# Table stores issued by ScalarE, the output tile of a table block as a step of its own, and the split of y one scan step later

## The chip, the cores and the metric

The kernel runs on one core of one Trainium2 chip. The metric is the device time of one execution in microseconds (us). A core has five engines that each run their own instructions in order: TensorE (PE in the profile; PEld is its weight load), VectorE (DVE), ScalarE (ACT), GpSimd (POOL) and SyncE (SP). They meet through semaphores. Transfers are issued by SP, ScalarE or GpSimd and run on DMA engines that the whole core shares.

## The reference

A decoder trunk of two layers on x of 256 positions by 2048 features in float32. Each layer ends in `layer_norm(alpha * x + mixer(x))`.

```
def ssd_moba_mixer(x, w_in, conv_w, conv_b, dt_bias, a_log, d_skip, norm_g, w_out):   # layer 0
    z, xbc, dt, q, k, v, gate = jnp.split(x @ w_in, SPLITS0, axis=-1)
    ...                                   # conv, chunked state-space scan, RMSNorm -> y_a
    y_b = moba_attention(q, k, v).reshape(bsz, s, ATT_WIDTH) * jax.nn.silu(gate)
    return jnp.concatenate([y_a, y_b], axis=-1) @ w_out

def s5_ssm(u, lam_re, lam_im, log_dt, b_re, b_im, c_re, c_im, d_skip):
    lam = lax.complex(lam_re, lam_im); dt = jnp.exp(log_dt)[:, None]
    lam_bar = jnp.exp(lam * dt)
    b_bar = ((lam_bar - 1.0) / lam)[..., None] * lax.complex(b_re, b_im)
    c_mat = lax.complex(c_re, c_im)
    def step(h, u_blk):                   # 128 groups of 16 channels, 64 complex states each
        bu = jnp.einsum('gnm,blgm->blgn', b_bar, u_blk)
        bu = bu.at[:, 0].add(lam_bar * h)
        _, hs = lax.associative_scan(_linear_recurrence, (lam_bar, bu), axis=1)
        return hs[:, -1], jnp.einsum('gmn,blgn->blgm', c_mat, hs).real
    ...
    return y + d_skip * u

def s5_mixer(x, w_in, ..., w_glu, w_out):                                              # layer 1
    u, gate = jnp.split(x @ w_in, 2, axis=-1)
    y = jax.nn.gelu(s5_ssm(u, ...))
    ga, gb = jnp.split(y @ w_glu, 2, axis=-1)
    return ((ga * jax.nn.sigmoid(gb)) * jax.nn.silu(gate)) @ w_out
```

## The kernel before

**Products.** The time goes into five large products (`wi0`, `wo0`, `wi1`, `wglu`, `wo1`). [...] Weights come in units of 128 partitions by 1024 float32 (512 KB). SP loads a unit into `raw` (L222), ScalarE makes the upper part `wh` (L225) and VectorE the remainder `wl` (L227). There are four buffers of each, and `split_to` prepares units up to three ahead of the one that TensorE works on. The matmuls of the products stand at L271 (one unit is 12 of them, 512 columns each) and L288 (24 of them, 256 columns each). The large tiles that hold split activations have the one-letter names A, B, C, D, F.

**Side work.** All else is cut into small jobs. `pump`, called after each unit, takes some of them. Jobs in the queue `jobs` are spread over the product at hand; jobs in the queue `back` are spread evenly over the units up to a unit number, `goal`. So a job more in `back` changes beside which unit the later ones are issued. The order on each engine is then settled by a scheduler that simulates the kernel's times; an engine executes its own list strictly in that order.

**Scan tables, made during layer 0.** Layer 1 needs tables for its scan that depend on parameters alone. They are built in 16 blocks, b = 0 to 15, as jobs in `back`, in `block_jobs(b)`, and go to DRAM, into `wb[b]`:

- `bars` loads the parameters (L650) and makes `bb`.
- `efs` makes `et` (L676 to L679, VectorE) and, in the same job, the second half of the output tile `ob` (L684 to L686, VectorE). `ob` has two buffers, so the tile of block b can be written only after the store of block b−2 has landed.
- `pes` transposes `et` on TensorE (L694, with 16 small matmuls at L698), copies the result into the first half of `ob` on ScalarE (L699), makes `kt` on VectorE (L704, L705) and stores `ob` (L706, 512 KB), issued by GpSimd.
- `mts`, for odd b, makes `om` from `kt` on TensorE (L713), VectorE (L715) and ScalarE (L717) and stores its two halves (L719, 128 KB each), issued by GpSimd.

GpSimd also computes a table of phasors for each block (L627 to L640), a chain of small products (L630, L635, L637, L638) that ends with a store of its own (L640). The blocks run beside the attention and the output product of layer 0. At the end of layer 0 comes a LayerNorm whose four column quarters are normalized (L1010, L1013), transposed on TensorE (L358) and split on ScalarE (L1023) and VectorE (L1027), while the first product of layer 1 has begun.

**The scan in layer 1.** A list of steps, `at(t, f)`, is spread over the units of the first product of layer 1. For block b it loads the tables (L1111, step 2b−2), encodes on TensorE (L1128, step 2b), rotates on VectorE (up to L1146), scans there (L1153, L1155, L1156), decodes on TensorE (L1169, L1173, step 2b+3), applies GELU on ScalarE (L1179) and stores to `yd` (L1184, L1185). u goes through DRAM: `u_store` (L1083, L1084) writes a quarter of it and `u_load` (L1094, L1095) reads it back in another layout as `um`. y comes back the same way: when the four blocks of a quarter are done, `y_load` (L1198) reads it into a tile and `y_split` divides it into upper part (L1206, ScalarE, into A) and remainder (L1207, VectorE, into B). The tile of `y_load` and that of `u_store` are one buffer (tag `ut`).

Of the kernel before, what the change touches and what calls it, by code (L numbers as in the profile page):

```python
# [9 lines left out]
F32 = mybir.dt.float32  # L10
# [6 lines left out]
P = 128  # L17
# [142 lines left out]
def trunk(tc, io, out):  # L160
    nc = tc.nc
# [3 lines left out]
    def nm(s):  # L165
        count[0] += 1
        return f"{s}_{count[0]}"

    with ExitStack() as top:
# [10 lines left out]
        def C(name):  # L180
            lo, hi = CONST[name]
            return ct[:, lo:hi]

        def PR(name):
            lo, hi = PARAM[name]
            return pt[:, lo:hi]
# [3 lines left out]
        def aux():  # L190
            return auxp.tile([P, 512], F32, tag="aux", name=nm("aux"))

        def big(tag, shape, dt=F32):
            return slot.tile(shape, dt, tag=tag, name=nm(tag))
# [176 lines left out]
        wb = [dram.tile([P, 1792], F32, name=f"wb{b}") for b in range(16)]  # L371
# [9 lines left out]
        with ExitStack() as l0:  # L381
            wk = l0.enter_context(tc.tile_pool(name="wk", bufs=1))
            pp = l0.enter_context(tc.tile_pool(name="pp", bufs=1))
# [260 lines left out]
            def block_jobs(b):  # L644
                h = {}
                gs = slice(8 * b, 8 * b + 8)

                def bars():
                    bc = h["bc"] = pp.tile([P, 4, 8, 16], F32, tag="bc", name=nm("bc"))
                    nc.sync.dma_start(bc.rearrange("p a g m -> p (a g m)"), io["s5bc"][b].rearrange("p a g m -> p (a g m)"))  # L650
                    bb = h["bb"] = pp.tile([P, 3, 8, 16], F32, tag="bb", name=nm("bb"))
                    tm = pp.tile([P, 512], F32, tag="tm", name=nm("tm"))
                    tv = tm.rearrange("p (a g m) -> p a g m", a=4, g=8)
                    wr = wri[:, 0, gs].unsqueeze(2).to_broadcast([P, 8, 16])
                    wi = wri[:, 1, gs].unsqueeze(2).to_broadcast([P, 8, 16])
                    V.tensor_tensor(bb[:, 0], bc[:, 0], wr, op=OP.mult)
                    V.tensor_tensor(tv[:, 0], bc[:, 1], wi, op=OP.mult)
                    V.scalar_tensor_tensor(bb[:, 1], bc[:, 1], sgn, wr, op0=OP.mult, op1=OP.mult)
                    V.scalar_tensor_tensor(tv[:, 1], bc[:, 0], sgn, wi, op0=OP.mult, op1=OP.mult)
                    V.tensor_tensor(bb[:, 0], bb[:, 0], tv[:, 0], op=OP.add)  # L660
                    V.tensor_tensor(bb[:, 1], bb[:, 1], tv[:, 1], op=OP.subtract)
                    V.tensor_scalar(bb[:, 2], bc[:, 2], nsg, None, op0=OP.mult)

                def lk(i, k):
                    return lam[:, i, gs, k - 1].unsqueeze(2).to_broadcast([P, 8, 16])

                def fk(i):
                    return lap[:, i, 4 * b : 4 * b + 4, :].unsqueeze(2).to_broadcast([P, 4, 16, 4])

                def efs():  # L670
                    bc, bb = h["bc"], h["bb"]
                    et = h["et"] = pp.tile([P, 8, 16, 4], F32, tag="et", name=nm("et"))
                    tm = pp.tile([P, 8, 16, 4], F32, tag="tm", name=nm("tm"))
                    ob = h["ob"] = pp.tile([P, 1024], F32, tag="ob", bufs=2, name=nm("ob"))
                    for s in range(3):
                        V.tensor_tensor(et[:, :, :, s], bb[:, 0], lk(0, 3 - s), op=OP.mult)  # L676
                        V.tensor_tensor(tm[:, :, :, s], bb[:, 1], lk(1, 3 - s), op=OP.mult)
                    V.tensor_tensor(et[:, :, :, 0:3], et[:, :, :, 0:3], tm[:, :, :, 0:3], op=OP.add)
                    V.tensor_copy(et[:, :, :, 3], bb[:, 0])  # L679
                    cp = [bc[:, 3, 4 * i : 4 * i + 4, :].unsqueeze(3).to_broadcast([P, 4, 16, 4]) for i in range(2)]  # L680
                    for r in range(2):
                        fv = ob[:, 512 + 256 * r : 768 + 256 * r].rearrange("p (g m t) -> p g m t", g=4, m=16)
                        tm = pp.tile([P, 4, 16, 4], F32, tag="tm", name=nm("tm"))
                        V.tensor_tensor(fv, cp[0], fk(r), op=OP.mult)  # L684
                        V.tensor_tensor(tm, cp[1], fk(1 - r), op=OP.mult)
                        V.tensor_tensor(fv, fv, tm, op=OP.add if r else OP.subtract)  # L686

                def pes():
                    et, ob, bb = h["et"], h["ob"], h["bb"]
                    ev = et.rearrange("p (a i) m s -> p a (i m s)", i=2)  # L690
                    cv = bb[:, 2].rearrange("p (a i) m -> p a i m", i=2)
                    pe, pk = aux(), aux()
                    for a in range(4):
                        T.transpose(pe[:, a * P : a * P + P], ev[:, a, :], ident)  # L694
                    for a in range(4):
                        for i in range(2):
                            at = 64 * (i ^ (a % 2))
                            T.matmul(pk[at : at + 64, a * 16 : a * 16 + 16], ev[:, a, 64 * i : 64 * i + 64], cv[:, a, i, :], start=True, stop=True)  # L698
                    A.activation(ob[:, 0:512], pe, AF.Copy)  # L699
                    if b % 2 == 0:  # L700
                        ktp[0] = pp.tile([P, 8, 16], F32, tag="kt", name=nm("kt"))
                    kt = ktp[0][:, 4 * (b % 2) : 4 * (b % 2) + 4, :]
                    dc = PR("s5d")[:, 4 * b : 4 * b + 4].unsqueeze(2).to_broadcast([P, 4, 16])
                    V.tensor_tensor(kt, C("kmask").unsqueeze(1).to_broadcast([P, 4, 16]), dc, op=OP.mult)  # L704
                    V.tensor_tensor(kt, pk[:, 0:64].rearrange("p (a m) -> p a m", m=16), kt, op=OP.add)  # L705
                    nc.gpsimd.dma_start(wb[b][:, 0:1024], ob)  # L706

                def mts():
                    kf = ktp[0].rearrange("p a m -> p (a m)")
                    pm = aux()  # L710
                    om = pp.tile([P, 512], F32, tag="om", name=nm("om"))
                    for j in range(3):
                        T.matmul(pm[:, j * 128 : j * 128 + 128], C("shift")[:, j * P : j * P + P], kf, start=True, stop=True)  # L713
                    mv = om.rearrange("p (k t) -> p t k", t=4)
                    V.tensor_copy(mv[:, 3, :], kf)  # L715
                    for j in range(3):
                        A.activation(mv[:, 2 - j, :], pm[:, j * 128 : j * 128 + 128], AF.Copy)  # L717
                    for i in range(2):
                        nc.gpsimd.dma_start(wb[b - 1 + i][:, 1024:1280], om[:, 256 * i : 256 * i + 256])  # L719

                return [bars, efs, pes, mts] if b % 2 else [bars, efs, pes]

            jobs.extend([trig_job, table_job])
            xs = big("C", [P, 2, D])
# [344 lines left out]
        with ExitStack() as l1:  # L1069
# [18 lines left out]
            def u_load(hh):  # L1088
                j, h = hh // 2, hh % 2
                u = um[hh] = w1("um", [P, 12, 64], 3)  # L1090
                for i in range(2):
                    src = ud[j][16 * h + 8 * i : 16 * h + 8 * i + 8].rearrange("q a c -> a q c")
                    at = 64 * (1 - i)
                    nc.gpsimd.dma_start(u[64 * i : 64 * i + 64, 0:8, :], src)  # L1094
                    nc.gpsimd.dma_start(u[at : at + 64, 8:12, :], src[:, 1::2, :])  # L1095
# [3 lines left out]
            def at(t, f):  # L1099
                steps.setdefault(t, []).append(f)  # L1100
# [99 lines left out]
            def y_split(j):  # L1200
                if j == 0:
                    y5["h"] = big("A", [P, KT, S], F32R)
                    y5["l"] = big("B", [P, KT, S], F32R)
                yt = y5[j]
                fs = slice(4 * j, 4 * j + 4)
                A.activation(y5["h"][:, fs, :], yt, AF.Copy)  # L1206
                V.tensor_tensor(y5["l"][:, fs, :], yt, y5["h"][:, fs, :].bitcast(F32), op=OP.subtract)  # L1207

            for b in range(16):
                ssm(b)  # L1210
                if b % 2 == 0:
                    at(2 * b - 2, lambda b=b: u_load(b // 2))
                if b % 4 == 3:
                    at(2 * b + 6, lambda b=b: y_load(b // 4))
                    at(2 * b + 8, lambda b=b: y_split(b // 4))
            sg1 = wk.tile([P, 2, D], F32, tag="sg1", bufs=1, name="sg1")
            for j in range(8):
                ps = product("w" if j < 4 else "x", x1hl) if j else first1
# [105 lines left out]
```

## Time and profile before

| | |
|---|---|
| median of 3 runs | 1374.88 us |
| lowest and highest run | 1372.33 and 1376.38 us |
| profiled execution, its own time | 1374.04 us |
| its span | 1372.3 us |
| TensorE busy | 1351.2 us (98%) |
| VectorE busy | 980.6 us (71%) |
| ScalarE busy | 673.5 us (49%) |
| GpSimd busy | 372.2 us (27%) |
| issued by SP (q1) | 239.33 MB |
| issued by GpSimd (q0) | 40.90 MB |
| issued by ScalarE (q10) | 1.18 MB |

How to read the rows that follow. A row of the timeline is: start in us, duration in us, engine, line of the kernel, instruction, output<-inputs, sizes, how many times, and in brackets how long the engine had been idle and what released it. Matmuls are pipelined, so their durations overlap and one reads the distance from start to start. A row of the waits is: engine, output and line, what it waited for, then us in total, times, and the longest. A row of the windows is: the stretch in us, its length, then busy time and number of instructions of PE, PEld, DVE, ACT and POOL, then TensorE's granted clock (1.00 is full speed), the DMA engines' busy share and GB/s. A row of the chain that ended last is: start, duration, and what the chain went through there. In a group of one line's instructions, three durations are minimum, median and maximum in ns. A row of the DMA issues ends with the size and the median time from issue to landing in us.

### The profile page before, as it was taken

The page shows a single profiled execution, that of the slowest core. Times are in us where ns is not written, and L with a number is a line of the kernel's source. Part 1 is how long each engine was busy: PE and PEld are TensorE (multiplying, and loading weights), DVE is VectorE, ACT ScalarE, POOL GpSimd, SP SyncE. Part 2 cuts the span into 40 slices and gives each one's busy share as a digit, 9 for nine tenths or more (in the row PEclk, how much of TensorE's full clock was granted, in tenths as well). Part 3 has the DMA queues.
Part 4 walks back from the last instruction along what each step waited for, and adds up shares of the span by engine and source line. Part 5 has one row for each costly group of instructions (what it writes and reads, how often), then busy time and mean ns, then how long its engine had stood idle before and what let it go on. Part 6 is the DMA issues. An engine that isn't in the chain of part 4 may idle for free.

```text
span 1372.3 us, 25096 instructions
## 1 busy us (share of the span) xinstructions
PE 1351.2 (98%) x9918; PEld 1216.1 (89%) x9918; DVE 980.6 (71%) x1559; ACT 673.5 (49%) x869; POOL 372.2 (27%) x681
## 2 busy tenths in 40 slices
PE   9999999999999999999999899999999999999996
PEld 9999999998998998998988788899877788888885
DVE  5788746787688789779877766748878856555665
ACT  5565557754544544544554344344345545444441
POOL 0140000122016637737888200013333200000001
PEclk9999999999999999999999999999999999999998
DMA  8556655445546756755866678498889766666772
GB/s 304 179 156 197 182 169 155 160 146 171 174 150 209 240 175 214 234 182 190 278 193 194 221 226 305 143 304 264 278 225 303 219 207 186 197 184 187 256 216 77
DMA packets 79206, 283.02 MB, mean 206 GB/s; under 512 B 9840, under 2 KB 10480, under 8 KB 78576
## 3 DMA queue, kind: packets, MB, share of 16 engines
q1 hardware_dynamic: 68112, 239.33, 56.1%
q0 software_dynamic: 10400, 40.90, 8.8%
q8 instruction: 78, 1.28, 0.4%
q10 hardware_dynamic: 576, 1.18, 0.2%
q14 instruction: 40, 0.33, 0.1%
HBM read 260.41 MB, written 20.97 MB: 205 GB/s over the span
## 4 chain that ended last, share of the span: by engine, by line
PE 85%; POOL 7%; DVE 3%; DMA 2%; issue 2%; ACT 0%; POOLq 0%
PE main L288 42%; PE main L271 35%; POOL c L635 3%; POOL c L637 1%; POOL c L638 1%; DMA wb<-c 1%; PE aux L358 1%; DVE wl L227 1%; PE aux L791 1%; PE enc L1128 1%; PE dec L1173 1%; PE aux L367 1%; DMA ut<-yd 1%; PE aux L761 0%; PE aux L698 0%
## 5 line engine op out<-in xcount | busy, mean ns | idle before, releaser
L227 DVE TENSOR_TENSOR wl<-raw,wh 128x1024 fp32r<-128x1024 f32 x431 | 537.3, 1248 | 334.7 <-ACT wh L225 328.7
L225 ACT ACTIVATE wh<-raw 128x1024 fp32r<-128x1024 f32 x431 | 455.8, 1059 | 581.0 <-PE main L271 270.7
L288 PE MATMUL main<-A,wh 128*128 128x256 f32 x1408 | 402.5, 286 | 0.0
L288 PE MATMUL main<-A,wl 128*128 128x256 f32 x1408 | 400.1, 284 | 0.0
L288 PE MATMUL main<-B,wh 128*128 128x256 f32 x1408 | 399.8, 284 | 0.0
L288 PEld LDWEIGHTS main<-A,wh 128*128 128x128 f32 x1408 | 270.5, 192 | 0.6 <-issue 0.2
L288 PEld LDWEIGHTS main<-B,wh 128*128 128x128 f32 x1408 | 270.5, 192 | 0.4
L288 PEld LDWEIGHTS main<-A,wl 128*128 128x128 f32 x1408 | 270.5, 192 | 0.3 <-issue 0.2
L271 PE MATMUL main<-wh,A 128*128 128x512 f32 x512 | 201.5, 394 | 0.0
L271 PE MATMUL main<-wh,B 128*128 128x512 f32 x512 | 201.1, 393 | 0.0
L271 PE MATMUL main<-wl,A 128*128 128x512 f32 x512 | 200.9, 392 | 0.0
L271 PE MATMUL main<-wh,C 128*128 128x512 f32 x384 | 152.4, 398 | 0.0
L271 PE MATMUL main<-wh,F 128*128 128x512 f32 x384 | 150.5, 392 | 0.0
L271 PE MATMUL main<-wl,C 128*128 128x512 f32 x384 | 150.3, 391 | 0.0
L271 PEld LDWEIGHTS main<-wh,B 128*128 128x128 f32 x512 | 96.7, 189 | 20.2
L271 PEld LDWEIGHTS main<-wl,A 128*128 128x128 f32 x512 | 96.8, 189 | 20.0 <-issue 0.2
L271 PEld LDWEIGHTS main<-wh,A 128*128 128x128 f32 x512 | 96.7, 189 | 19.9 <-issue 0.2
L635 POOL TENSOR_TENSOR c<-c 128x8 f32<-128x8 f32 (+2 forms) x192 | 99.3, 535 | 19.2 <-DMA wb<-c 11.8
L271 PEld LDWEIGHTS main<-wh,C 128*128 128x128 f32 x384 | 72.5, 189 | 15.7
L271 PEld LDWEIGHTS main<-wh,F 128*128 128x128 f32 x384 | 72.4, 188 | 15.3
L271 PEld LDWEIGHTS main<-wl,C 128*128 128x128 f32 x384 | 72.5, 189 | 14.5
L801 POOL TENSOR_TENSOR ssq<-ssq,c 128x256 f32<-128x256 f32 x16 | 17.6, 1100 | 210.2 <-ACT c L799 209.6
(281 smaller groups left out, 1690.0 us busy)
## 6 DMA issues: line engine op xcount, KB each, us to landing
raw<-in_wi SPq DMA_DIRECT2D x271, 512.0 KB, 4.1
raw<-in_wo SPq DMA_DIRECT2D x96, 512.0 KB, 4.3
raw<-in_wglu SPq DMA_DIRECT2D x64, 512.0 KB, 3.7
wt<-wb POOLq DMA_DIRECT2D x16, 896.0 KB, 8.1
wb<-ob POOLq DMA_DIRECT2D x16, 512.0 KB, 6.0
bc<-in_s5bc SPq DMA_DIRECT2D x16, 256.0 KB, 4.2
wb<-c POOLq DMA_DIRECT2D x16, 256.0 KB, 3.6
wb<-om POOLq DMA_DIRECT2D x16, 128.0 KB, 3.4
```

The source lines that it names most:

```text
L225: high = A.activation(wh, raw, AF.Copy)
L227: splits[n] = (high, V.tensor_tensor(wl, raw, wh.bitcast(F32), op=OP.subtract))
L271: T.matmul(ps[o], l[:, k, sl], r[:, j, :], start=start and i == 0, stop=stop and i == 2)
L288: T.matmul(pv[o // 2][:, o % 2, :], l[:, j, sl], r[:, k, :], start=first and i == 0 and o % 2 == 0, stop=end and i == 2 and o % 2 == 1, sk ...
L358: end = T.transpose(dst[:, i * P : i * P + P], s, ident)
L367: T.matmul(px[:64, 0:64], idle, idle, start=i == 0, stop=i == n - 1)
L635: G.tensor_tensor(p[:, :, :, 0:m], cs[:, :, :, 1 : m + 1], cs[:, i, :, n : n + 1].unsqueeze(1).to_broadcast([P, 2, 4, m]), op=OP.mult)
L637: G.tensor_tensor(cs[:, 0, :, n + 1 : n + 1 + m], p0[:, 0, :, 0:m], p1[:, 1, :, 0:m], op=OP.subtract)
L638: G.tensor_tensor(cs[:, 1, :, n + 1 : n + 1 + m], p0[:, 1, :, 0:m], p1[:, 0, :, 0:m], op=OP.add)
L791: T.matmul(yo, xs[:, 0, xc], df[:, i, 0:256], start=True, stop=False)
L801: G.tensor_tensor(ssq, ssq, jk[:, f, :], op=OP.add)
L1128: T.matmul(px[64 * at : 64 * at + 64, i, r * 128 + q * 64 : r * 128 + q * 64 + 64], wt[64 * i : 64 * i + 64, a * P + 64 * r : a * P + 64 * ...
```

## The change

Three edits. The stores of `ob` (L706) and `om` (L719) are issued by ScalarE instead of GpSimd; the phasors' store L640 stays on GpSimd. The part of `efs` that makes the second half of `ob` becomes a job of its own, `fcs`, between `efs` and `pes`, so that the tile is taken there; 16 more jobs stand in `back` with that, 97 instead of 81, up to the same unit. `y_split` moves from step 2b+8 to 2b+9 of the scan's list. No arithmetic changes. The diff:

```diff
@@ efs, in block_jobs
                     tm = pp.tile([P, 8, 16, 4], F32, tag="tm", name=nm("tm"))
-                    ob = h["ob"] = pp.tile([P, 1024], F32, tag="ob", bufs=2, name=nm("ob"))
                     for s in range(3):
                         V.tensor_tensor(et[:, :, :, s], bb[:, 0], lk(0, 3 - s), op=OP.mult)
                         V.tensor_tensor(tm[:, :, :, s], bb[:, 1], lk(1, 3 - s), op=OP.mult)
                     V.tensor_tensor(et[:, :, :, 0:3], et[:, :, :, 0:3], tm[:, :, :, 0:3], op=OP.add)
                     V.tensor_copy(et[:, :, :, 3], bb[:, 0])
+
+                def fcs():
+                    bc = h["bc"]
+                    ob = h["ob"] = pp.tile([P, 1024], F32, tag="ob", bufs=2, name=nm("ob"))
                     cp = [bc[:, 3, 4 * i : 4 * i + 4, :].unsqueeze(3).to_broadcast([P, 4, 16, 4]) for i in range(2)]
                     for r in range(2):
                         fv = ob[:, 512 + 256 * r : 768 + 256 * r].rearrange("p (g m t) -> p g m t", g=4, m=16)
@@ pes
-                    nc.gpsimd.dma_start(wb[b][:, 0:1024], ob)
+                    nc.scalar.dma_start(wb[b][:, 0:1024], ob)
@@ mts
                     for i in range(2):
-                        nc.gpsimd.dma_start(wb[b - 1 + i][:, 1024:1280], om[:, 256 * i : 256 * i + 256])
-
-                return [bars, efs, pes, mts] if b % 2 else [bars, efs, pes]
+                        nc.scalar.dma_start(wb[b - 1 + i][:, 1024:1280], om[:, 256 * i : 256 * i + 256])
+
+                return [bars, efs, fcs, pes, mts] if b % 2 else [bars, efs, fcs, pes]
@@ layer 1
                 if b % 4 == 3:
                     at(2 * b + 6, lambda b=b: y_load(b // 4))
-                    at(2 * b + 8, lambda b=b: y_split(b // 4))
+                    at(2 * b + 9, lambda b=b: y_split(b // 4))
```

Lines of the kernel before are given throughout the prediction; from `fcs` on those of the changed kernel are three higher.

## The prediction

> **What bounds the kernel now.** I read the page's busy shares first, then the waits, then a table of windows, and last the timeline around each wait of TensorE (PE).
>
> ```profile
> span 1372.3 us, 25096 instructions
> PE 1351.2 (98%) x9918; PEld 1216.1 (89%) x9918; DVE 980.6 (71%) x1559; ACT 673.5 (49%) x869; POOL 372.2 (27%) x681
> ACT wh L225 <- PE main L271: 270.7, 167, 6.8
> PE dec L1173 <- DVE gt L1155: 2.9, 1, 2.9
> 750.00:775.00 25.00, 20.87 (x97) 16.80 (x96) 13.65 (x24) 7.78 (x10) 12.63 (x33) 0.86 0.74 253
> 1000.00:1025.00 25.00, 22.08 (x231) 16.81 (x231) 21.95 (x32) 12.66 (x15) 7.77 (x15) 0.93 0.77 236
> ```
>
> PE is busy for 98% of the span. ScalarE (ACT), which makes the upper half `wh` of every weight unit, mostly waits for PE to hand a buffer back (270.7 us in 167 waits), so time is gained only where PE stops or runs slowly. In the middle of the kernel there are two such places, one in each of the two windows shown: PE is busy 20.87 and 22.08 us of 25, and its mean granted clock (the column behind POOL) is 0.86 and 0.93. The change touches what stands behind both.
>
> **Part 1: the stores and the split of `efs`.** The first place, in the timeline, with two rows of the chain of waits at the end:
>
> ```profile
> 737.99 0.39 PE L271 MATMUL main<-wh,C 128*128 128x512 f32 x1
> 738.86 0.60 ACT L699 ACTIVATE ob<-aux 128x512 f32<-128x512 f32 x1 [1.64 <-PE aux L694]
> 739.33 0.50 PE L271 MATMUL main<-wl,C 128*128 128x512 f32 x1
> 739.99 0.42 DVE L686 TENSOR_TENSOR ob<-ob,tm 128x256 f32<-128x256 f32 x1
> 750.66 0.55 POOL L706 DMA_DIRECT2D wb<-ob  x1
> 754.65 0.39 PE L271 MATMUL main<-wh,B 128*128 128x512 f32 x1
> 756.72 1.58 DVE L684 TENSOR_TENSOR ob<-bc,lap 128x256 f32<-128x256 f32 x2 [5.11 <-DMA wb<-ob]
> 758.23 0.80 DVE L678 TENSOR_TENSOR et<-et,tm 128x384 f32<-128x384 f32 x1
> 759.17 1.05 PE L694 MATMUL aux<-consts,et 128*128 128x128 f32 x4 [4.13 <-DVE et L678]
> 761.13 0.80 PE L271 MATMUL main<-wh,A 128*128 128x512 f32 x1
> 766.25 0.40 PE L271 MATMUL main<-wh,A 128*128 128x512 f32 x1
> 750.66 6.04 DMA wb<-ob
> 818.36 49.92 PE main L271 x220
> ```
>
> The `ob` of one block is complete at 739.99+0.42 = 740.41, but GpSimd (POOL), which works through its phasor products in order, issues the store at 750.66: 10.25 us of queue, then 6.04 us of transfer. VectorE (DVE) stands at the next write into that buffer (L684) for 5.11 us, and the planner has put L684 ahead of L678, the sum that completes `et`. So L678 is late, PE's transposes L694 wait 4.13 us, and afterwards PE runs at about half clock.
>
> Price: from the last product matmul before the table group to the first after it takes 761.13−754.65 = 6.48 us; the same group without a wait takes 739.33−737.99 = 1.34; so 5.14 us. Then 12 product matmuls take 766.25−761.13 = 5.12 us; at the 49.92/220 = 0.227 us of the long run they take 2.72; so 2.40. Together **7.54 us**.
>
> After: ScalarE issues the store when its own L699 (738.86+0.60) and VectorE's L686 are done, at about 740.4. Even with the 6.04 us of before it lands at 746.5. VectorE comes to L684 at 756.72−5.11 = 751.6: 5 us of slack, so the wait goes. The split cures it a second way, since the new step starts after `et` is complete and a late buffer no longer delays L678. Next late in that group would be L678 itself, done 0.8 us after the end of L677, before PE gets there. I take all 7.54.
>
> **Part 2: `y_split` one step later.** The second place, again with one row of the chain at the end:
>
> ```profile
> 990.65 0.39 PE L271 MATMUL main<-wh,F 128*128 128x512 f32 x1
> 991.07 1.06 ACT L225 ACTIVATE wh<-raw 128x1024 fp32r<-128x1024 f32 x1 [1.66 <-PE main L271]
> 991.36 0.75 POOL L1198 DMA_DIRECT2D ut<-yd  x1 [5.81 <-DMA ud<-ut]
> 991.82 0.50 PE L271 MATMUL main<-wh,C 128*128 128x512 f32 x1
> 998.89 1.06 ACT L1206 ACTIVATE A<-ut 128x1024 fp32r<-128x1024 f32 x1 [6.76 <-DMA ut<-yd]
> 1000.74 0.39 PE L271 MATMUL main<-wh,F 128*128 128x512 f32 x1
> 1005.50 0.79 PE L271 MATMUL main<-wh,C 128*128 128x512 f32 x1
> 1008.54 0.39 PE L271 MATMUL main<-wl,C 128*128 128x512 f32 x1
> 991.36 7.50 DMA ut<-yd
> ```
>
> The load of the first quarter of y is issued at 991.36 and lands at 998.86. ScalarE has stood at its split L1206 for 6.76 us by then, with the weight splits L225 queued behind it; VectorE's half L1207 and the scan's L1155 come later still, and PE's L1173 waits 2.92 us. Price: 1005.50−1000.74 = 4.76 against 991.82−990.65 = 1.17 for the like group, so 3.59; then 7 matmuls in 1008.54−1005.50 = 3.04 against 7×0.227 = 1.59, so 1.45. Together **5.04 us**.
>
> After: in the changed order two more weight splits stand ahead of L1206 on ScalarE. They come at PE's pace of 12×0.227 = 2.72 us, at 993.8 and 996.5, so ScalarE reaches L1206 at about 997.6 and waits 1.3 us instead of 6.76. What is queued behind is the next `wh`; the buffers ahead hold 3×2.72 us of PE's work, less 1.06 for `wh` and 1.22 for `wl`, so 5.9 us of cover. L1155 stands ahead of L1207 on VectorE now. The wait of PE goes; I take all 5.04.
>
> **Part 3: what is new.**
>
> ```profile
> L1299 ACTq DMA_DIRECT2D out_x<-D x4: 338/338/377, 1355.4 to 1368.3; - x4
> DMA to landing us min/median/max: 3.7/6.0/7.8
> POOL wb L706 <- DVE kt L705: 53.7, 3, 24.3
> 873.52 0.44 PE L358 MATMUL aux<-consts,D 128*128 128x128 f32 x2 [1.27 <-DVE D L1013]
> 875.00:879.00 4.00, 4.00 (x23) 4.00 (x22) 3.54 (x6) 0.36 (x1) 0.00 (x0) 0.57 0.00 0
> 882.44 1.04 PE L358 MATMUL aux<-consts,D 128*128 128x128 f32 x8
> 883.80 1.22 DVE L227 TENSOR_TENSOR wl<-raw,wh 128x1024 fp32r<-128x1024 f32 x1
> 884.93 0.68 DVE L1027 TENSOR_TENSOR F<-aux,C 128x512 fp32r<-128x512 f32 x1
> 979.94 0.96 PE main L288 x8
> 912.14 0.72 POOL L1094 DMA_DIRECT2D um<-ud  x1 [4.98 <-DMA ud<-ut]
> 920.50 0.32 PE L1128 MATMUL enc<-um,wt 64*64 64x64 f32 x2
> um<-ud POOLq DMA_DIRECT2D x16, 128.0 KB, 6.2
> ```
>
> *Issue on ScalarE.* 16 table stores and 16 small ones at 0.34 us each (first row, ScalarE's own issue) are 10.8 us on an engine at 49%; the 1.66 us of idle before a weight split takes one. Path cost 0. Without that cover it would be 10.8. GpSimd loses the same 32 issues, which are on no path; only its wait for kt (third row, 53.7 us) goes with them.
>
> *Wait on ScalarE.* The store waits for VectorE's L686 (about 1 us in the rows of Part 1) and has L225 queued behind it; cover 5.9 us; cost 0. The trace has no large store on ScalarE's queue: 3.7 to 7.8 us to landing (second row, the table stores on GpSimd's) are the nearest bounds, and with any of them the buffer is free in time.
>
> *Layer 0's LayerNorm tail.* The 16 additional steps shift the planner's order at 882 us: all 8 transposes L358 come after 48 product matmuls, and the product then needs the fourth L1027, which stands on VectorE behind the `wl` of a unit whose `wh` waits for the last of these matmuls. That chain is 1.06 (`wh`) + 1.22 + 0.68 = 3.0 us against 1.04 of transposes and two matmuls at 0.96/8 = 0.12 (the row at 979.94, of the chain) of cover: a wait of about 1.7 us that is not there now, less some 0.3 from transposes that move behind matmuls: +1.4. A wait of 1.27 us at 873.52 was followed by a clock of 0.57 over 4 us, a loss of 4×0.43 = 1.7. Loss of clock 0 to 1.7, taken 0.7: **+2.1** (bounds 0 to 3.1).
>
> *First encoding.* L1128 comes 20 matmuls (2.4 us) earlier in the new order. Its input is issued at 912.14, median landing 6.2, so 918.3 to 918.6; needed at 920.50 now and 918.1 after. **+0.7** (0 to 2.4).
>
> **Sum.** The profiled execution took 1374.04 us (span 1372.3 and 1.7 around it): 1374.04−7.54−5.04+2.1+0.7 = 1364.3. The median of the runs stands 0.84 above it; forecast 1365.1.
>
> [...] The rows show 10.25 us of queueing ahead of 6.04 us of transfer. [...]
>
> The granted clock fell after PE waits of 4.13, 2.92 and 1.27 us. [...]
>
> **Rivals.**
> - *A, the forecast*: 1365.1. For it: both chains are seen from end to end, each with slack of 4 us or more after the change.
> - *B, the y load is later than reckoned* (it shares DMA engines with the table loads), and 5.9 us of cover don't do: only Part 1 is saved, 1374.88−7.54+2.8 = 1370.1. Against: it would have to land after 1003.
> - *C, the store lands no earlier*, since it shares the DMA engines with the weight loads: only Part 2 is saved, 1374.88−5.04+2.8 = 1372.6. Against: it would need over 11 us where 7.8 is the longest of 16, and `et` no longer waits. [...]
> - *D, ScalarE is held by its stores.* It runs in order, and a store that waits for VectorE's part of `ob` keeps back every later `wh`. It decides from a hold of 5.9 us; then PE stops, with its half clock, for the like of Part 1, 7.54 us. For: GpSimd stood at this store for up to 24.3 us for VectorE (kt), and the new step can be placed late. Against: ScalarE comes to it only after its own L699, and L686 was 1 us later. One such block: 1365.1+7.5 = 1372.6; three: 1365.1+22.6 = 1387.7.
>
> **How the numbers follow.** A 0.65, B 0.10, C 0.05, D with one block 0.06, with two or more 0.14. A change under 0.3% (4.1 us) is about what can't be told from none here. Faster, below 1370.8: A and 0.06 of B, 0.71. Same: the rest of B, C and D with one block, 0.15. Slower: D with more, 0.14. The range goes from 1360.0 (both new costs at nothing is 1362.3, and the fastest run of before lay 2.5 under its median) to 1372.6, which holds B, C and D's first block; only D's rest and the tails lie outside. For A alone: 1360 to 1368.
>
> **What would show it.** In the waits after, PE <- et and PE <- gt L1155 gone or under 0.5 us; VectorE's wait at L684 gone; the windows at 750 and 1000 at a clock of 1.00; a new PE wait for L1027 near 880 of 1 to 2 us. A wait of ScalarE for L686 of over 3 us, or PE's idle time growing between 400 and 820 us, would make it wrong; so would a long wait at L1206.

## The result and the profile after

The changed kernel took 1364.68 us (median of 4 runs, 1362.64 to 1366.41) against 1374.62 for the kernel before (4 runs, 1372.33 to 1376.38): a ratio of 0.9927, 95% interval 0.9915 to 0.9940. The forecast was 1365.1 in 1360.0 to 1372.6. Timed again in another set it took 1365.29 (6 runs) against 1373.16, a ratio of 0.9934 (0.9919 to 0.9949). The profiled execution took 1366.41 us, the longest of the four; its span was 1364.6.

First the page's head, the waits and the windows of the kernel after, which answer to those of before. Columns are as there.

```profile
span 1364.6 us, 25068 instructions
PE 1349.1 (99%) x9918; PEld 1214.1 (89%) x9918; DVE 982.8 (72%) x1559; ACT 673.3 (49%) x869; POOL 372.3 (27%) x649
```

```profile
PE aux L358 <- DVE D L1016: 1.4, 2, 1.3
PE main L288 <- DVE F L1030: 0.9, 1, 0.9
PE main L288 <- ACT C L1026: 0.6, 2, 0.3
PE main L271 <- DVE wl L227: 0.3, 1, 0.3
ACT A L1209 <- DMA ut<-yd: 0.6, 2, 0.4
```

```profile
750.00:775.00 25.00, 25.00 (x129) 20.70 (x129) 17.22 (x30) 10.46 (x13) 21.52 (x45) 1.00 0.77 233
1000.00:1025.00 25.00, 25.00 (x253) 19.58 (x252) 21.72 (x32) 11.73 (x13) 7.82 (x15) 1.00 0.87 282
855.00:905.00 50.00, 47.09 (x348) 44.66 (x347) 32.21 (x47) 16.95 (x25) 4.15 (x9) 0.93 0.55 195
```

In the waits, TensorE's 4.1 us for `et` and 2.9 us for `gt` are gone, and VectorE's wait at the tile write does not appear. In the windows at 750 and 1000, TensorE is busy for the whole 25 us at full clock. What is left stands at the LayerNorm tail (third window, clock 0.93): a new wait of 0.88 us for L1030 (L1027 of before), and two of about 0.3 for L1026.

**Where the time went, place by place.** All traces hold the same 7680 product matmuls, some 50 of them in another place in the kernels with the split and in e7 (six in e5 and e10), none across a bound of the table, so one can compare when the n-th of them starts. The table gives, for each profiled execution, how much longer or shorter a stretch was than in the kernel before (us). The stretches run from product matmul 0 to 4872 (734 us in the kernel before), to 4968 (the table group of the first place), to 5760 (end of layer 0, LayerNorm, start of layer 1 with the first encoding), to 6144, to 6264 (the second place), and to the end.

| kernel | to 4872 | first place | LayerNorm tail | scan | second place | rest |
|---|---|---|---|---|---|---|
| changed | +1.29 | −7.43 | +3.55 | 0.00 | −4.95 | −0.09 |
| changed, again (e9) | +1.28 | −7.43 | +3.71 | 0.00 | −4.95 | −0.09 |
| stores alone (e1) | +0.30 | −7.43 | +0.38 | 0.00 | +2.57 | −0.01 |
| split alone (e2) | +0.98 | +3.82 | +1.04 | 0.00 | −0.06 | 0.00 |
| y_split alone (e3) | −0.32 | −0.47 | +0.01 | 0.00 | −4.95 | −0.09 |
| stores and y_split (e4) | +0.39 | −7.43 | +0.51 | 0.00 | −4.95 | −0.09 |
| the same, stores on SP (e6) | +0.23 | −7.43 | +0.02 | 0.00 | −4.95 | +0.05 |
| split and y_split (e8) | +1.05 | +3.33 | +1.03 | 0.00 | −4.95 | −0.09 |
| tile made in `pes` (e5) | +0.30 | −7.43 | −0.29 | 0.00 | −4.95 | −0.09 |
| tile made in `pes`, again (e10) | −0.75 | −7.43 | −0.84 | 0.00 | −4.94 | −0.10 |
| store held by GpSimd (e7) | +12.99 | −7.43 | +3.57 | 0.00 | −4.95 | −0.09 |

e5 and e10 are one kernel. Their first column differs by 1.05, and 1.04 of that has arisen by product matmul 174, long before the first table block; at the tail they differ by 0.55. Differences of that size between two rows need no cause in the kernel.

### The profile page after: what moved, and what is told of

Same layout as the page of the kernel before. It is cut to its first block, busy times and chain, and to the rows that moved or that the text cites. A ratio compares the mean times of both kernels' runs of the same rounds, so it can differ in the third digit from the quotient of the medians.

```text
span 1364.6 us, 25068 instructions
## 1 busy us (share of the span) xinstructions
PE 1349.1 (99%) x9918; PEld 1214.1 (89%) x9918; DVE 982.8 (72%) x1559; ACT 673.3 (49%) x869; POOL 372.3 (27%) x649
## 3 DMA queue, kind: packets, MB, share of 16 engines
q8 instruction: 78, 1.28, 0.4%
## 4 chain that ended last, share of the span: by engine, by line
PE 94%; DVE 4%; DMA 1%; issue 1%; ACT 0%; POOL 0%; POOLq 0%; DVEq 0%
PE main L288 43%; PE main L271 43%; DVE wl L227 1%; PE aux L358 1%; PE enc L1131 1%; PE aux L794 1%; PE dec L1176 1%; PE aux L701 1%; PE aux L367 1%; DMA bc<-in_s5bc 1%; PE aux L906 1%; PE aux L874 1%; PE aux L764 0%; PE dec L1172 0%; PE aux L697 0%
## 5 line engine op out<-in xcount | busy, mean ns | idle before, releaser
L227 DVE TENSOR_TENSOR wl<-raw,wh 128x1024 fp32r<-128x1024 f32 x431 | 538.5, 1251 | 329.5 <-ACT wh L225 323.4
L288 PE MATMUL main<-A,wh 128*128 128x256 f32 x1408 | 402.6, 286 | 0.0
L288 PE MATMUL main<-B,wh 128*128 128x256 f32 x1408 | 400.1, 284 | 0.0
L288 PE MATMUL main<-A,wl 128*128 128x256 f32 x1408 | 399.9, 284 | 0.0
L288 PEld LDWEIGHTS main<-A,wh 128*128 128x128 f32 x1408 | 270.8, 192 | 0.6 <-issue 0.2
L288 PEld LDWEIGHTS main<-B,wh 128*128 128x128 f32 x1408 | 270.8, 192 | 0.4
L288 PEld LDWEIGHTS main<-A,wl 128*128 128x128 f32 x1408 | 270.7, 192 | 0.2 <-issue 0.2
L635 POOL TENSOR_TENSOR c<-c 128x8 f32<-128x8 f32 (+2 forms) x192 | 108.0, 581 | 28.8 <-DMA wb<-c 21.3
L271 PEld LDWEIGHTS main<-wh,C 128*128 128x128 f32 x384 | 72.1, 188 | 15.5
```

The lines of the kernel that those rows point to most:

```text
L227: splits[n] = (high, V.tensor_tensor(wl, raw, wh.bitcast(F32), op=OP.subtract))
L271: T.matmul(ps[o], l[:, k, sl], r[:, j, :], start=start and i == 0, stop=stop and i == 2)
L288: T.matmul(pv[o // 2][:, o % 2, :], l[:, j, sl], r[:, k, :], start=first and i == 0 and o % 2 == 0, stop=end and i == 2 and o % 2 == 1, sk ...
L635: G.tensor_tensor(p[:, :, :, 0:m], cs[:, :, :, 1 : m + 1], cs[:, i, :, n : n + 1].unsqueeze(1).to_broadcast([P, 2, 4, m]), op=OP.mult)
```

## The experiments

The theory: the first place is GpSimd's queue, the second is the time of `y_split`, and what is paid for it is a shift of the planner's order. The rivals: the split is what frees the first place; the issuing engine matters little; ScalarE is held by its stores. The edits are against the kernel before unless said.

**e1, the stores alone.** 1369.68 us (10 runs, 1364.21 to 1371.71); ratio 0.9962 (0.9949 to 0.9975).

```diff
-                    nc.gpsimd.dma_start(wb[b][:, 0:1024], ob)
+                    nc.scalar.dma_start(wb[b][:, 0:1024], ob)
...
-                        nc.gpsimd.dma_start(wb[b - 1 + i][:, 1024:1280], om[...])
+                        nc.scalar.dma_start(wb[b - 1 + i][:, 1024:1280], om[...])
```

> Only the stores of ob and om move to ScalarE; efs stays whole, y_split stays at its step. Theory (the queue behind GpSimd's phasors is the cause at the first place): the store goes out within 1 us of the end of ob, VectorE's wait at L684 and PE's wait of 4.1 us at L694 are gone, the stretch loses the 7.4 us that it lost in the changed kernel: 1374.6 - 7.4 = 1367.2, with the second place as before (wait of 2.9 us for gt). Rival (only the split frees et; the issuing engine matters little since the transfer takes its 6 us in any case): L684 still waits and L694 with it, 1374.6 within 2.

The first place gave its 7.43 us with the stores alone, so the split is not needed for it. The total is 2.5 short of the expectation since the second place became worse by 2.57. Its waits and its row in the chain:

```profile
PE dec L1173 <- DVE gt L1155: 3.7, 1, 3.7
PE dec L1169 <- ACT ys L1179: 1.6, 1, 1.6
985.49 9.06 DMA ut<-yd
```

The load of y took 9.06 us to land here against 7.50 in the kernel before, and against TensorE's own progress it was issued some 0.9 us later, so it landed about 2.4 us later in all. ScalarE stood longer at `y_split`, and now two steps of the scan were late. With `y_split` at its old step, a later landing of this load is paid almost in full (2.57). The ten executions spread from 1364.21 to 1371.71; only the profiled one can be read this way.

**e2, the split alone.** 1380.99 us (6 runs, 1379.11 to 1384.94); ratio 1.0052 (1.0034 to 1.0070): slower than before.

```diff
+                def fcs():
+                    bc = h["bc"]
+                    ob = h["ob"] = pp.tile([P, 1024], F32, tag="ob", bufs=2, name=nm("ob"))
...
-                return [bars, efs, pes, mts] if b % 2 else [bars, efs, pes]
+                return [bars, efs, fcs, pes, mts] if b % 2 else [bars, efs, fcs, pes]
```

> Only fcs is split from efs; the stores stay on GpSimd, y_split stays at its step. Theory: et no longer stands behind the tile, so PE's wait at L694 goes, but VectorE still stands some 5 us at L684 and wl of the next units behind it, which the 5.9 us of cover just hold; and the shift of the order costs about 3.6 us at the LayerNorm tail and 1.3 in the attention stretch: 1374.6 - 7.4 + 4.9 = 1372.1. Rival (the hold of VectorE then stops PE through wl): the 7.4 stay and the shift is paid on top, 1379.5.

The rival won, and the first place even grew (+3.82), where the rival left it as it was. Its rows in this kernel's timeline (L687 is L684 of before):

```profile
757.22 0.60 PE L697 MATMUL aux<-consts,et 128*128 128x128 f32 x4
764.70 0.58 POOL L709 DMA_DIRECT2D wb<-ob  x1
767.66 1.06 DVE L687 TENSOR_TENSOR ob<-bc,lap 128x256 f32<-128x256 f32 x2 [15.52 <-DMA wb<-ob]
770.24 0.79 PE L271 MATMUL main<-wl,A 128*128 128x512 f32 x1 [8.68 <-DVE wl L227]
```

The transposes of `et` no longer wait, as intended. But the store leaves GpSimd only at 764.70, VectorE stands for 15.52 us at the tile instead of 5.11, and the weight remainders L227 queued behind it stop TensorE for 8.68 us. The wait has moved from `et` to `wl` and grown.

**e3, y_split alone.** 1368.81 us (6 runs, 1368.03 to 1370.14); ratio 0.9959 (0.9944 to 0.9973).

```diff
-                    at(2 * b + 8, lambda b=b: y_split(b // 4))
+                    at(2 * b + 9, lambda b=b: y_split(b // 4))
```

> Only y_split comes one step later. Theory: ScalarE waits under 1.5 us for the y tile, PE's wait for gt goes with its half clock, 1374.6 - 5.0 = 1369.6. Rival (the clock does not fall after 2.9 us of waiting, so only the wait counts): 1374.6 - 3.6 = 1371.0.

The second place gave 4.95 of the 5.04 worked out, more than the 3.6 of the rival, so the half clock is part of it: from 985 to 1020 us the mean clock is 1.00 here and 0.95 in the kernel before.

**e4, stores and y_split, without the split.** 1362.24 us (6 runs, 1361.21 to 1363.57); ratio 0.9912 (0.9896 to 0.9928). The edits are those of e1 and e3.

> Stores on ScalarE and y_split one step later, but efs whole as before. Theory: both places are cured without the split, and PE's order at the LayerNorm tail stays that of the kernel before, so the split's cost is spared: 1374.6 - 7.4 - 5.0 = 1362.2, some 2.5 below the changed kernel. Rival (the split carries part of the gain): above 1364.7, up to 1369.6 if the stores alone do nothing.

Both places are cured, and the tail costs +0.51 instead of +3.55.

**e8, split and y_split, stores on GpSimd.** 1375.44 us (10 runs, 1374.41 to 1377.21); ratio 1.0009 (0.9999 to 1.0018). The edits are those of e2 and e3.

> The changed kernel with its stores back on GpSimd: split and later y_split alone. Theory (split alone measured 1381.0, the later y_split takes off 5.0 to 5.5): 1375.7, so no gain over the kernel before, with PE's wait of about 9 us for wl near 760. Rival (the split was to free et and the stores are secondary): 1370 or less.

Without the move of the stores the rest of the change brings nothing: the second place's 4.95 are paid back at the first one (+3.33), the tail (+1.03) and ahead of them (+1.05). TensorE's wait for `wl`, as expected:

```profile
PE main L271 <- DVE wl L227: 8.9, 2, 8.4
```

Beside the changed kernel's 1364.68 the move is worth 10.8 us here.

**e6, the stores on SP.** 1362.34 us (5 runs, 1362.19 to 1362.61); ratio 0.9913 (0.9899 to 0.9928). The edit to e4:

```diff
-                    nc.scalar.dma_start(wb[b][:, 0:1024], ob)
+                    nc.sync.dma_start(wb[b][:, 0:1024], ob)
...
-                        nc.scalar.dma_start(wb[b - 1 + i][:, 1024:1280], om[...])
+                        nc.sync.dma_start(wb[b - 1 + i][:, 1024:1280], om[...])
```

> As the version without the split (stores moved, y_split later, efs whole), but the stores are issued by SP, whose queue also issues all weight loads. Theory (the cause was GpSimd's queue, any queue that is not held will do): 1362.2 within 1.5, since a weight load that stands 1 to 3 us behind a store's wait has up to three units of 2.7 us ahead of it. Rival (weight loads held behind the stores come late): waits of ScalarE for raw in the table stretch and 1365 or more.

The same time as with ScalarE. What matters is that the queue is not GpSimd's.

**e5 and e10, the tile's second half in `pes`.** 1361.58 us (5 runs, 1360.45 to 1363.21), ratio 0.9907 (0.9894 to 0.9921); beside the changed kernel on the same chip 1360.15 (4 runs, 1359.98 to 1361.08), ratio 0.9901 (0.9886 to 0.9917). The edit to the changed kernel:

```diff
-                def fcs():
-                    ...                              # ob, L684 to L686
 def pes():
+                    ob = h["ob"] = pp.tile([P, 1024], F32, tag="ob", bufs=2, name=nm("ob"))
 ...
                     V.tensor_tensor(kt, pk[:, 0:64].rearrange("p (a m) -> p a m", m=16), kt, op=OP.add)
+                    ...                              # L684 to L686
                     nc.scalar.dma_start(wb[b][:, 0:1024], ob)
...
-                return [bars, efs, fcs, pes, mts] if b % 2 else [bars, efs, fcs, pes]
+                return [bars, efs, pes, mts] if b % 2 else [bars, efs, pes]
```

> Stores on ScalarE, y_split later; the tile's second half is made in pes, after kt, instead of in a job of its own, so there are 81 jobs as before and PE's order at the LayerNorm tail is that of the kernel before. On ScalarE each store stands right behind its copy L692 and now has to wait for six VectorE operations that come after kt, 2 to 5 us. Theory (the split's cost is the shifted tail order, and a hold of ScalarE under 5.9 us is covered): 1362.2 within 1.5. Rival (ScalarE held by its stores stops PE): waits of PE for wl or wh appear in the table stretch, 2 us or more each, 1370 or more.

> The tile's second half made in pes after kt, stores on ScalarE, y_split later, beside the changed kernel on the same chip. Theory: 1361.6, no wait of PE left but the 1.3 us at the head of the LayerNorm tail. Rival: as the changed kernel within 1 us.

> The changed kernel itself, timed beside the next one on the same chip, to measure what the split's shifted order costs. Theory (wait of PE for L1030 and the slow clock at the LayerNorm tail, some 3 us): 1364.7, about 0.9927 of before, and above the version with the tile made in pes by 2 to 3.5 us. Rival (the two are the same kernel to PE): within 1 us of each other.

These are the lowest medians, though the interval of e5 overlaps those of e4 and e6. On the same chip (e10 beside e9) this version stands 5.1 us under the changed kernel (1360.15 against 1365.29), more than the 2 to 3.5 expected, and their runs don't overlap (1361.08 at most against 1363.43 at least). The stores do hold ScalarE, which issues one only when VectorE's part of the tile is made. The longest hold in e5, from the end of the copy to the store:

```profile
755.13 0.60 ACT L692 ACTIVATE ob<-aux 128x512 f32<-128x512 f32 x1
759.67 0.33 ACTq L707 DMA_DIRECT2D wb<-ob  x1
```

This hold of 3.94 us costs TensorE nothing: all its waits in e5 (over 0.25 us) are those of the first LayerNorm transposes and the start. That the tile's part comes after `et` is thus free here, where the order of the tail is that of the kernel before.

**e7, ScalarE's store made to wait for GpSimd.** A single execution, 1378.13 us, so without an interval. The edit to e4 is an operation more per block, a copy of four columns onto themselves:

```diff
+                    G.tensor_copy(ob[:, 1020:1024], ob[:, 1020:1024])
                     nc.scalar.dma_start(wb[b][:, 0:1024], ob)
```

> As the version without the split, with one operation added per block: GpSimd copies four columns of ob onto themselves before ScalarE's store, so that the store, with the weight splits behind it on ScalarE, waits for GpSimd's queue. In the kernel before, the stores stood in that queue for 26 to 36 us in three blocks and 6 to 11 us in five. Theory of the cover: a hold under 5.9 us costs PE nothing; of a longer one PE pays the rest and some 2.4 us of half clock. Worked out with the three long ones and two of the others: 20 + 30 + 15 + 5 + 4 and 5 x 2.4, so about 1362 + 86 = 1448; if the planner's order shortens them, 1400. Rival (ScalarE's place has slack of its own): under 1375.

Both expectations missed. The holds were shorter than the store's longest stays in GpSimd's queue in the kernel before (36, 26 and 21 us), and the cover was longer than 5.9 us. The longest and the third longest hold, and TensorE's start after the longest:

```profile
652.23 0.59 ACT L699 ACTIVATE ob<-aux 128x512 f32<-128x512 f32 x1
661.39 0.33 ACTq L707 DMA_DIRECT2D wb<-ob  x1
680.86 0.58 ACT L699 ACTIVATE ob<-aux 128x512 f32<-128x512 f32 x1
696.45 0.33 ACTq L707 DMA_DIRECT2D wb<-ob  x1
697.98 0.80 PE L271 MATMUL main<-wh,A 128*128 128x512 f32 x1 [5.59 <-ACT wh L225]
```

From 652.82 to 661.39 ScalarE stood for 8.57 us and TensorE did not wait. From 681.44 to 696.45 it stood for 15.01, and TensorE waited 5.59 for `wh` and 0.46 for `wl` behind it. A hold of 9.21 us that ended at 554.33 was followed, at 557.20, by the one wait for `wl` among the products at L288:

```profile
PE main L288 <- DVE wl L227: 0.7, 1, 0.7
```

So rival D's mechanism exists, and its point lies near 9 us in this stretch, not at 5.9. The stretch up to the first place became 12.99 us longer; the waits hold 6.8 of that. The first product matmul after the longest wait took 0.80 us (the last row) where those ahead of the wait took 0.39 to 0.40, which points to a slower clock as part of the rest; how much was not taken apart.

## Why the prediction was right, point by point

**The bound and the two places** were right: −7.43 at the first (worked out: 7.54), −4.95 at the second (5.04), half clock included. That the median came within 0.4 us of the forecast is partly luck: the profiled execution lay 2.1 us above its sum, and the median, which was put 0.84 above the profiled execution, lay 1.73 below it.

**One step in Part 1 was wrong, though its result stands.** The prediction put the store issued at 750.66 to the `ob` complete at 740.41, and so read 10.25 us of queue. `ob` has two buffers, so the tile that L684 writes at 756.72 takes the buffer of two blocks earlier. The write of the tile between them, and the copy that completed the earlier one, are these rows of the kernel before:

```profile
714.50 0.58 ACT L699 ACTIVATE ob<-aux 128x512 f32<-128x512 f32 x1
731.51 0.68 DVE L684 TENSOR_TENSOR ob<-bc,lap 128x256 f32<-128x256 f32 x1
```

The store issued at 750.66 is that of the copy that ended at 715.08: it stood in GpSimd's queue for 35.6 us, not 10. After the change, the timeline shows the same store and the same write:

```profile
718.44 0.60 ACT L702 ACTIVATE ob<-aux 128x512 f32<-128x512 f32 x1 [2.22 <-PE aux L697]
719.07 0.33 ACTq L709 DMA_DIRECT2D wb<-ob  x1
752.33 0.86 DVE L687 TENSOR_TENSOR ob<-bc,lap 128x256 f32<-128x256 f32 x2
```

It is issued 0.03 us after the copy, and the slack to the write at 752.33 is some 28 us with the 5.5 us of the median landing, not 5. The wrong pairing made the margin look small; the direction did not hang on it.

**"The split cures it a second way"** failed. e2 shows what it does with the store still late: the wait passes from `et` to `wl` and costs more. The prediction named the cover of VectorE's queue nowhere; behind L684 stand weight remainders, and 15.5 us exceed what lies ready. With the stores moved, the split only costs.

**What is new** was right in kind and mis-sized. In the profiled execution the terms were:
- the LayerNorm tail +3.55, worked out as +2.1 with bounds of 0 to 3.1, so outside them. The waits were sized rightly: TensorE's waits there grew from 1.6 us (L358) to 2.9 (L358, L1030 and L1026), +1.3 against +1.4. The clock was not: it fell to half twice instead of once, each time for 3.41 us, which is up to 1.7 more where 0.7 was taken. Some 0.5 was not traced. The second fall, in windows:

```profile
876.13:879.54 3.41, 2.04 (x15) 1.39 (x13) 3.41 (x6) 1.90 (x3) 0.00 (x0) 1.00 0.62 171
879.54:882.95 3.41, 3.41 (x19) 3.41 (x18) 3.36 (x6) 0.00 (x0) 0.00 (x0) 0.50 0.43 142
```

- the stretch before the first place +1.29, worked out as nothing. In the shifted order VectorE's `wl` is late at 434 and 538 us, where the products start about 0.3 and 0.7 us late in all. Another 0.38 arises in the first 174 product matmuls, where all the kernels lie between −0.38 and +0.75. The rest was not traced.
- the first encoding 0.00, worked out as +0.7: TensorE does not wait there.

1374.04 − 7.43 − 4.95 + 3.55 + 1.29 − 0.09 = 1366.41, the profiled execution's time. So the 2.1 us by which it lies above the 1364.3 of the sum are the tail (1.45 more), the earlier stretch (1.3) and the two places (0.2 less gained), less the encoding (0.7) and the rest (0.1).

**The cost of the split** in all is 1364.68 against 1362.24 without it (e4, another set), and 1365.29 against 1360.15 with the same tile work after `et` and the old order of the tail (e9, e10); of the latter two, the profiled executions have a mean clock of 0.93 against 1.00 in the window of 855 to 905 us. That it is the order and not the number of jobs is seen in e7, which has 81 jobs and pays +3.57 at the tail: there TensorE's transposes stand at the same product matmuls as in the changed kernel. That the added operations did this by moving the planner's times is the likely reason, not a shown one.

**Rival C** did not come about: the first place gave 7.43 us. The store's landing itself was hardly faster, 5.5 us in the median from ScalarE against 6.0 from GpSimd:

```profile
L709 ACTq DMA_DIRECT2D wb<-ob x16: 326/327/355, 412.4 to 808.7; - x16
DMA to landing us min/median/max: 3.2/5.5/8.3
```

What the move took away is the 35.6 us for which the store stood behind other work of its engine; a store on SP (e6) gives the same 7.43 us.

**Rival B** did not come about in the changed kernel, where ScalarE waits 0.4 us at most at L1209. e1 shows that the y load can be later than reckoned: it took 9.06 us to land against 7.50 in the kernel before, 1.6 longer. That it is the table loads that delay it was not shown. **Rival D** did not either, but the sign that the prediction gave for it came: it took the hold of ScalarE at a store as about 1 us and called one of over 3 us a sign of being wrong. In three blocks ScalarE stood for 3.41, 3.80 and 4.10 us until VectorE's L689 (L686 of before) was done. The longest, from 541.09 to 545.20:

```profile
540.49 0.60 ACT L702 ACTIVATE ob<-aux 128x512 f32<-128x512 f32 x1 [1.36 <-PE aux L697]
544.67 0.43 DVE L689 TENSOR_TENSOR ob<-ob,tm 128x256 f32<-128x256 f32 x1
545.20 0.33 ACTq L709 DMA_DIRECT2D wb<-ob  x1
545.62 2.01 ACT L225 ACTIVATE wh<-raw 128x1024 fp32r<-128x1024 f32 x2 [4.53 <-PE main L271]
```

TensorE's waits list none for `wh`, and the one for `wl`, at 538.82, comes before this hold. The cost of 0 stood, since the cover was longer than the hold and not because the hold was short.

## What to carry to other kernels

When an engine waits for a buffer, find the transfer that frees it, count back by the number of buffers to the work that it stores, and compare the time at which that was complete with the time of issue: a long gap is the issuing engine's queue, and a queue that is not held will do (here ScalarE's and SP's alike). Splitting a step to let its urgent half pass does not help while the other half can still stand at the head of an engine that feeds the critical one; cure the wait itself, and then see whether the split is still wanted. Where a planner sets the order, count a small reshuffle as an edit with a price of its own: here 2 to 5 us between medians, most of it at a LayerNorm tail that no line of the change touches.

## What was not expected of the hardware

What the clock costs after a wait of TensorE is not fixed here by the length of the wait, nor by the kernel. At the LayerNorm tail every kernel has a wait of 1.27 to 1.3 us and some others, yet the mean clock of the same 50 us differs. One window of each of these, in this order: the tile in `pes` (e10), the same kernel in its other set (e5), the kernel before, and the split alone (e2):

```profile
855.00:905.00 50.00, 47.98 (x392) 46.37 (x391) 32.61 (x47) 18.27 (x25) 5.58 (x12) 1.00 0.59 212
```

```profile
855.00:905.00 50.00, 48.51 (x384) 46.89 (x383) 33.21 (x48) 17.33 (x24) 3.75 (x10) 0.97 0.57 203
```

```profile
855.00:905.00 50.00, 48.37 (x353) 45.56 (x352) 33.69 (x49) 17.97 (x24) 3.33 (x8) 0.97 0.60 208
```

```profile
855.00:905.00 50.00, 46.45 (x325) 42.31 (x324) 35.81 (x50) 20.02 (x26) 2.92 (x8) 1.00 0.57 203
```

A loss of 0.03 is what one stretch of 3.41 us at half clock comes to in 50 us, as the kernel before has it from 875.26 us on; that of 0.07 in the changed kernel is two. e10 and e5 run the same program, and one execution keeps a mean clock of 1.00 where the other has 0.97. The split alone has the longer waits in this window (1.3 us twice) and the full clock; its tail costs +1.04, that of the changed kernel, with the same order, +3.55.

In the traces of the kernel before and of the changed one, all changes of clock lie whole steps of 3.413 us apart: in the kernel before, the three falls in the middle begin at 759.21, 875.26 and 1004.97 us, 34 and 38 steps apart. At the tail the clock fell after short waits: in the window of 855 to 905 us, read in every kernel but e7, it is 1.00 in e2, e8 and e10, 0.93 in the changed kernel (both times) and 0.97 in the other six, with no wait of TensorE at the tail longer than 1.3 us. In the step of 3.41 us ahead of a fall at the tail TensorE was busy for 1.78 us in the kernel before (871.85 to 875.26), and for 1.87 (865.89 to 869.30) and 2.04 in the changed one. Over the whole 50 us the busy time does not decide: the split alone was busy for 46.45 us and kept the full clock, the kernel before for 48.37 and did not. What decides, the length of a wait, its place in the step or the kind of matmul, no run here tells; it stays open.
